# Hybrid encoder, two layers: the second half's leading products taken from unnormalised tiles

## The chip, the cores and the metric

The kernel runs on one core of one Trainium2 chip. The core has a matrix engine (TensorE, in profiles PE), three engines for elementwise work (VectorE or DVE, ScalarE or ACT, GpSimd or POOL) and a queue engine (SyncE or SP) that issues most transfers. The metric is the device time of one execution in microseconds (us). Results of TensorE land in PSUM, eight banks of 128 x 512 float32 values; everything else lies in SBUF.

## The reference

Two layers of an encoder over 512 tokens of width 1024. Each layer has a token-mixing part and a channel-mixing part, each behind an RMS norm and followed by one:

```python
mem_n = rms_norm(mem, mem_norm_g)
for l in range(DEPTH):
    h = rms_norm(x, g_pre_mix[l])
    proj = h @ w_in[l]
    q_a, k_a, v_a, q_b, k_b, v_b, q_m, gate_pre = jnp.split(proj, splits, axis=-1)
    # o_a: 2-D neighbourhood attention, 6 heads; o_b: dilated attention, 6 heads;
    # o_m: attention of q_m into (mem_n @ w_mem_kv[l])
    gates = jax.nn.sigmoid(gate_pre.reshape(B, S, N_BRANCH, D) + b_gate[l])
    merged = (gates[:, :, 0] * (o_a @ w_br_a[l]) + gates[:, :, 1] * (o_b @ w_br_b[l])
              + gates[:, :, 2] * (o_m @ w_br_m[l]))
    x = x + rms_norm(merged @ w_out[l], g_post_mix[l])
    h = rms_norm(x, g_pre_ffn[l])
    u = depthwise_conv_centred(h @ w_up[l], conv_w[l], conv_b[l])
    a, b = jnp.split(u, 2, axis=-1)
    f = jax.nn.gelu(a) * b
    x = x + rms_norm(f @ w_down[l], g_post_ffn[l])
```

RMS norm divides a token's 1024 values by the root of their mean square and multiplies by a gain per channel. The factor of the division is one number per token (the token factor); since it is constant over the channels that a product sums over, `(x * gain * factor) @ w` equals `((x * gain) @ w) * factor`.

## The kernel before

**Layout.** Activations are held transposed: channels on the 128 partitions, tokens along the free dimension. The residual `x` is eight k tiles of 128 x 512 in two constant tensors. Many steps work on one half of the tokens (256, `HALVES`) at a time.

**Products.** Every float32 operand is split into a rounded part (`hi`, made by ScalarE) and its remainder (`lo`, made by VectorE or POOL), and `mm3` (line 244) replaces one product by three matmuls: hi x hi, hi x lo, lo x hi. Weights arrive by SP as 512 KB pieces into `wraw` (three buffers) and are split by `weights` (line 222) into `whi` and `wlo` (two buffers each), or into smaller `m`, `h` or `ka` tiles where they have to lie ready earlier. All matmuls are recorded at line 242, all transposes at line 253, and all ScalarE and VectorE instructions at line 114, so the profile's groups are told apart by tile names.

**Order of the work.** TensorE's order is fixed by the program: each of its instructions is chained behind the one before (`Woven.pe`, line 56). A clock `wv.clk` adds an estimated cost to each; jobs are generators that wait until a due time on this clock or until a flag is given. `wv.tick` (line 83), called after each k tile of a product, runs the jobs that are due. So the places of a job's matmuls between those of the projections come from the planner's estimates; when the engines come later than these, TensorE waits in order. `ready` (line 183) is a delay taken from estimated end times of ScalarE and VectorE. The order of the other engines' instructions within their queues is set when the program is built, and can differ from the order in the code.

**Token factors.** `rstd_job` (line 321) multiplies the sums of squares by a column of 1/1024 (`pt<-mean,...`), takes root and reciprocal (`st`), and spreads the factors over all partitions by two float32 matmuls per half: a column of `st`, read 128 times over, against the identity (`pt<-ident,st`). It runs 18 times in the program.

**The end of layer 0 and the start of layer 1.** `sublayer_end` (line 779) does w_down; its last m tile is done half by half. After each half an `end_job` (line 373) normalises the result (`og`, multiplied by the factors), adds it to `x`, and sums the squares of the new `x`; then `pre_norm_job` (line 359) computes the token factors for layer 1, multiplies `x` by gain and factor, and splits the result into `h` tiles (`normed`, line 340). Beside these stand the memory's keys and values (`mem_kv`, line 444; the value job `mem_v_job` transposes into score banks `s`). The memory's own norm is `mem_norm_job` (line 416): four loads on ScalarE's queue, eight squares on ScalarE, seven adds on POOL in layer 1, one `rstd_job`, and eight `normed`. It is started at the end of layer 0's up-projection.

**The leading products.** Layer 1 begins with six projections of neighbourhood attention whose weights are prepared ahead (`FIRST`, line 28; q, k and v of the first two head pairs). `run_group` (line 466) takes them two banks at a time: `mm, mm`, then `s, s`, then `o, pt`, 48 matmuls of 128 x 256 a pair; first for half 0, as soon as its `h` tiles are there, then for half 1. After that the six banks are read out (`a_q`, `a_k`, `a_v`, lines 528 to 550) and the other projections follow with both halves at once (`proj`, line 480). `a_v` copies values into one buffer `sq`, one part by ScalarE, two narrow parts by VectorE; `v_job` transposes it.

**A second form of norm, in the channel mixing.** `factor_end_job` (line 388) already gives out tiles with the gain but without token factors (`raw_split`, line 345); the up-projection takes them, and the factors, kept in a tile `R`, are multiplied to the results when these leave PSUM (`scaled`, line 354).

Of the kernel before, what the change touches and what calls it, by code (L numbers as in the profile page):

```python
# [14 lines left out]
SEQ = 512  # L15
# [12 lines left out]
FIRST = (0, 3, 6, 1, 4, 7)  # L28
# [91 lines left out]
def tile_hybrid_encoder(ctx, tc, xT, memT, memg, vecs, rpb, w_in, w_kv, w_bra, w_brb, w_brm,  # L120
# [238 lines left out]
    def pre_norm_job(l, goff, acc, hs, i):  # L359
        half, box = HALVES[i], []  # L360
        yield from rstd_job(acc if isinstance(acc, list) else [acc[:, half]], 256, box)
        for k in range(KD):
            normed(x[k][:, half], vec[:, l, goff + k:goff + k + 1], box[0], hs[k][0][:, half], hs[k][1][:, half],
                   G if k in LOG[l > 0 and goff == V_PRE] else V)
        crit[0] = last_copy[0]
        yield 1.2
        wv.give(f"h{l}.{goff}.{i}")
# [5 lines left out]
    def end_job(l, goff, og, acc, acc2, i, then, lat, more=()):  # L373
        half, box = HALVES[i], []
        yield lat
        yield from rstd_job([acc[:, half]] + list(more), 256, box)
        for k in range(KD):
            V.tensor_mul(og[k][:, half], og[k][:, half], box[0])
            (G if then is None and i and k in TAILG else V).tensor_add(x[k][:, half], x[k][:, half], og[k][:, half])
            if acc2 is not None:  # L380
                sumsq_add(acc2[:, half], x[k][:, half], k == 0, None, G if k in SQG[goff == V_POSTF] else V)
            else:
                nc.sync.dma_start(out=out[:, k, half], in_=x[k][:, half])
        if then is not None:
            yield 9.0
            yield from then(i)

    def factor_end_job(l, goff, og, acc, acc2, i, nxt):
# [5 lines left out]
        for k in range(KD):  # L394
            V.tensor_mul(og[k][:, half], og[k][:, half], box[0])
            V.tensor_add(x[k][:, half], x[k][:, half], og[k][:, half])
            raw_split(l, gnext, k, x[k][:, half], h[k][0][:, half], h[k][1][:, half])
            if k == 0:
                yield 0.6
            wv.give(f"h{l}.{gnext}.{i}.{k}")  # L400
            yield 1.05
        for k in range(KD):
            sumsq_add(acc2[:, half], x[k][:, half], k == 0)
# [4 lines left out]
        if i == 1:  # L408
            yield 0.6
            wv.give(f"R{l}.{gnext}")  # L410

# [51 lines left out]
    def group_banks():  # L463
        return [mmbank(), mmbank(), sbank(), sbank(), obank(128), tbank()]

    def run_group(grp, hs, half, flag, cols=None, side=2):
        if flag and side == 2:
            wv.need(flag)
        n = len(hs)
        ws, pss = grp  # L470
        for i in range(0, len(ws), side):
            for k in range(n):
                if flag and side > 2:
                    wv.need(f"{flag}.{k}")
                rhs = [t[:, half] for t in hs[k]]
# [66 lines left out]
    def a_v(ps, qkv, flag):  # L542
# [5 lines left out]
        V.tensor_copy(vv[:, 0, :, 8:16], ps3[:, :, 0:8])  # L548
        V.tensor_copy(vv[:, 0, :, 0:8], ps3[:, :, 56:64])
# [229 lines left out]
    def sublayer_end(l, goff, w_of, rhs, n_half, then, lat=(1.4, 1.8), mid=None, fill=()):  # L779
# [26 lines left out]
        for i, half in enumerate(HALVES):  # L806
# [12 lines left out]
            if isinstance(then, tuple):  # L819
# [5 lines left out]
    def first_squares(half):  # L825
        sqs = [ytile((128, 256)) for _ in range(KD)]
        for k in range(KD):
            ACT.activation(sqs[k], x[k][:, half], AF.Square)
# [17 lines left out]
    hm = []  # L846
# [3 lines left out]
    for l in range(depth):  # L850
        pss = group_banks()
        for i in range(2):
            run_group((gw, pss), hs, HALVES[i], f"h{l}.{V_PRE}.{i}")
# [5 lines left out]
        for pr in range(3):  # L859
            for i, evac in enumerate((a_q, a_k, a_v)):  # L860
                ps = pss[3 * pr + i] if pr < 2 else proj(l, 3 * i + pr, hs, fence if i < 2 else None)
# [38 lines left out]
        for i in range(2):  # L900
            run_group((gw, list(pss.values())), hs, HALVES[i], f"h{l}.{V_PREF}.{i}", None, 4)
# [41 lines left out]
        else:  # L943
            hm, km, vm = [], [], []
            wv.spawn(mem_norm_job(l + 1, hm, htile))
            box, pre = [], []

            def then(a, i, l=l, box=box):
                if i == 0:
                    box.extend(h_tiles())  # L950
# [16 lines left out]
            sublayer_end(l, V_POSTF, w_of, fs, 1, then, (1.4, LAT1), lambda: wv.spawn(kv_ahead()))  # L967
# [38 lines left out]
def _layout(inputs):  # L1006
# [13 lines left out]
    a["xT"] = np.ascontiguousarray(g["x"][0].T.reshape(KD, 128, SEQ).transpose(1, 0, 2))  # L1020
# [46 lines left out]
```

## Time and profile before

| | |
|---|---|
| median of three runs | 1564.54 us (1564.0 to 1566.41) |
| profiled execution | 1565.1 us, its span 1563.3 us |
| TensorE busy, matmuls | 1524.4 us, 7994 |
| VectorE, ScalarE, POOL busy | 945.2, 735.1, 155.2 us |
| mean granted TensorE clock | 0.994 of full speed |
| read from memory | 141.47 MB, 92 GB/s over the span |

A profile row gives the start and the length in us, the engine, the line, the operation, the tile written and those read (buffer numbers left out), the shapes and how many instructions of this kind are merged; in square brackets stands the idle time just before, and what ended it. Matmuls are pipelined, so two rows can overlap: the distance from start to start is what one costs in a stream. A float32 matmul appears as two records. A group's row ends in "busy, mean ns of one | idle before".

### The profile page before, as it was taken

To read this page: it belongs to the slowest core of one execution; us is meant where nothing else is said; L and a number is where in the kernel's file an instruction comes from. 1 tells how busy PE (TensorE), PEld (TensorE's weight loads), DVE (VectorE), ACT (ScalarE), POOL (GpSimd) and SP (SyncE) were. 2 spreads that over 40 slices of the span, in tenths; PEclk is the share of its full clock that TensorE was granted. 3 is DMA by queue.
4 is the path that set the end of the run, shared out by engine and by line. 5 is a ranking of instruction groups with operands and counts; after the bars stand their busy time and mean duration, and the time that the engine had idled before them with its cause. 6 is when DMAs were issued, how large, how long until landed. Compare 5 with 4: busy or idle time off the path is not lost.

```text
span 1563.3 us, 20698 instructions
## 1 busy us (share of the span) xinstructions
PE 1524.4 (98%) x7994; PEld 1303.7 (83%) x7994; DVE 945.2 (60%) x1682; ACT 735.1 (47%) x1267; POOL 155.2 (10%) x219
## 2 busy tenths in 40 slices
PE   6999999999999999999989999999999999999997
PEld 6888888888988888788889888888889888888887
DVE  6685566235777777742385856753456877775233
ACT  5564575236544444522344645743364544444231
POOL 4340000210000000100061400001100000000000
PEclk9999999999999999999989999999999999999999
DMA  7222113325113322333331221132250222333331
GB/s 244 88 79 72 61 57 96 93 95 163 54 56 101 100 94 95 104 98 101 115 115 44 80 69 63 56 108 81 95 189 15 81 95 95 94 100 96 98 103 63
DMA packets 46610, 144.90 MB, mean 93 GB/s; under 512 B 5232, under 2 KB 11376, under 8 KB 46512
## 3 DMA queue, kind: packets, MB, share of 16 engines
q1 hardware_dynamic: 44656, 139.61, 28.2%
q10 hardware_dynamic: 1152, 2.10, 0.5%
q0 software_dynamic: 704, 1.88, 0.4%
q8 instruction: 62, 1.02, 0.3%
q14 instruction: 36, 0.29, 0.1%
HBM read 141.47 MB, written 2.10 MB: 92 GB/s over the span
## 4 chain that ended last, share of the span: by engine, by line
PE 54%; DVE 3%; issue 0%; ACT 0%; ACTq 0%; DVEq 0%
PE mm L242 48%; PE s L242 3%; PE o L242 2%; PE pt L242 1%; PE pt L253 1%; DVE y L114 1%; DVE x L114 1%; DVE m L114 0%; DVE acc L114 0%; DVE wlo L114 0%; DVE ka L114 0%; DVE st L114 0%; ACT sq L114 0%; ACT y L114 0%; ACT m L114 0%
## 5 line engine op out<-in xcount | busy, mean ns | idle before, releaser
L242 PE MATMUL mm<-h,whi 128*128 128x512 f32 x2496 | 775.7, 392 | 0.0
L242 PEld LDWEIGHTS mm<-h,whi 128*128 128x128 f32 x2496 | 461.5, 188 | 90.9
L242 PE MATMUL mm<-h,wlo 128*128 128x512 f32 x1248 | 486.4, 390 | 0.0
L114 DVE TENSOR_TENSOR wlo<-wraw,whi 128x1024 fp32r<-128x1024 f32 (+1 forms) x213 | 259.8, 1221 | 293.9 <-ACT whi L114 291.5
L114 ACT CAST whi<-wraw 128x1024 fp32r<-128x1024 f32 (+1 forms) x213 | 221.0, 1039 | 318.5 <-PE mm L242 310.4
L242 PEld LDWEIGHTS mm<-h,wlo 128*128 128x128 f32 x1248 | 234.3, 188 | 49.9
L242 PE MATMUL mm<-m,whi 128*128 128x512 f32 (+1 forms) x800 | 216.3, 358 | 2.7 <-ACT whi L114 1.8
L242 PEld LDWEIGHTS mm<-m,whi 128*128 128x128 f32 x800 | 142.5, 190 | 25.1 <-ACT whi L114 2.2
L242 PE MATMUL mm<-m,wlo 128*128 128x512 f32 (+1 forms) x400 | 142.8, 357 | 1.2 <-DVE wlo L114 1.2
L114 DVE SCALAR_TENSOR_TENSOR y<-y,vec,y 128x511 f32<-128x511 f32 x176 | 130.9, 750 | 3.5 <-ACT y L114 0.9
L114 DVE TENSOR_TENSOR y<-mm,R 128x512 f32<-128x512 f32 x82 | 56.4, 688 | 68.5 <-PE mm L242 68.5
L242 PEld LDWEIGHTS mm<-m,wlo 128*128 128x128 f32 x400 | 75.9, 190 | 12.5 <-DVE wlo L114 1.6
L766 POOL TENSOR_TENSOR m<-m,y 128x512 f32<-128x512 f32 x28 | 36.1, 1288 | 405.7 <-DVE y L114 405.7
L114 ACT ACTIVATE y<-y,vec 128x512 f32<-128x512 f32 x88 | 71.0, 813 | 2.2 <-DVE y L114 1.9
L242 PE MATMUL mm<-m,m 128*128 128x512 f32 x240 | 63.6, 395 | 0.0
L114 ACT ACTIVATE y<-y 128x512 f32<-128x512 f32 x44 | 27.8, 632 | 72.0 <-DVE y L114 71.5
L242 PE MATMUL s<-h,m 128*128 128x256 f32 x384 | 54.7, 290 | 5.4 <-DVE m L114 5.4
L114 ACT ACTIVATE y<-mm,vec 128x512 f32<-128x512 f32 (+1 forms) x91 | 57.4, 631 | 0.1
L242 PE MATMUL mm<-h,m 128*128 128x256 f32 x360 | 54.6, 298 | 2.8 <-DVE h L114 1.8
L114 ACT CAST m<-pt 128x512 fp32r<-128x512 f32 (+1 forms) x72 | 38.2, 539 | 40.4 <-PE pt L253 32.0
L114 DVE TENSOR_TENSOR acc<-acc,sq 128x256 f32<-128x256 f32 (+1 forms) x80 | 40.5, 507 | 26.2 <-ACT sq L114 24.6
L114 DVE TENSOR_TENSOR m<-pt,m 128x512 fp32r<-128x512 f32 (+1 forms) x72 | 45.0, 629 | 18.3 <-ACT m L114 17.4
(143 smaller groups left out, 1762.5 us busy)
## 6 DMA issues: line engine op xcount, KB each, us to landing
wraw<-in_w_in_dram SPq DMA_DIRECT2D x88, 512.0 KB, 3.4
wraw<-in_w_up_dram SPq DMA_DIRECT2D x88, 512.0 KB, 3.3
wraw<-in_w_down_dram SPq DMA_DIRECT2D x32, 512.0 KB, 3.5
wraw<-in_w_out_dram SPq DMA_DIRECT2D x16, 512.0 KB, 4.2
wraw<-in_w_down_dram SPq DMA_DIRECT2D x16, 384.0 KB, 3.1
wraw<-in_w_kv_dram SPq DMA_DIRECT2D x8, 512.0 KB, 4.4
wraw<-in_w_bra_dram SPq DMA_DIRECT2D x16, 192.0 KB, 2.3
x<-in_xT_dram SPq DMA_DIRECT2D x8, 256.0 KB, 6.9
```

The source lines that it names most:

```text
L114: return op(*args, **kw)
L242: wv.pe(nc.tensor.matmul(ps, a, b, start=first, stop=last), cost)
L253: wv.pe(nc.tensor.transpose(ps[:, 128 * i:128 * i + 128], s, ident), 0.11)
L766: (V if br == 2 and m >= 6 else G).tensor_add(acc[m], acc[m], gs)
```

## The change

1. `rstd_job` spreads the factors with TensorE's transposes of the same 128-fold read column, at a planned cost of 0.11 instead of 0.22.
2. In layer 1 the second half's leading products read raw tiles. A new `raw_end_job` replaces `end_job` and `pre_norm_job` for half 1 at the end of layer 0: it updates `x`, splits `x` times gain into eight raw tiles of the `ka` kind (of which there are 12 buffers), gives a flag for each, sums the squares afterwards, copies the spread factors to `R`, and then makes the normalised `h` tiles as before, since all further projections need them. After the group, six VectorE instructions multiply the second half of the six banks by `R` in PSUM.
3. The six leading projections come in another order, so that the pairs are `mm, mm`, then `o, pt`, then `s, s`. Each projection keeps its kind of bank.
4. `mem_norm_job` for layer 1 starts 20 us of the planner's clock later.
5. `a_v`'s two narrow copies move from VectorE to ScalarE.
6. `x` is one tensor, half by half; the input is laid out to match, so that a load reads 2 KB in a row from each partition instead of twice 1 KB.

```diff
-FIRST = (0, 3, 6, 1, 4, 7)
+FIRST = (0, 3, 4, 7, 6, 1)
...
-    xs = [const.tile([128, 4, 512], F32, name=f"x{i}") for i in range(2)]
-    x = [xs[k // 4][:, k % 4, :] for k in range(KD)]
+    xs = const.tile([128, 2, KD, 256], F32, name="x")
+
+    def xh(k, half):
+        return xs[:, half.start // 256, k, :]
...
-            nc.sync.dma_start(out=xs[k // 4][:, k % 4:k % 4 + 2, half], in_=xT[:, k:k + 2, half])
+            i = half.start // 256
+            nc.sync.dma_start(out=xs[:, i, k:k + 2, :], in_=xT[:, i, k:k + 2, :])
...
-            mm(pr[:, 128 * b:128 * b + 128], spread, ident, True, True, 0.22)
+            wv.pe(nc.tensor.transpose(pr[:, 128 * b:128 * b + 128], spread, ident), 0.11)
...
+    def raw_end_job(l, goff, og, acc, acc2, nxt, lat):
+        half, box = HALVES[1], []
+        hs, raw, R = nxt
+        yield lat
+        raw.extend((t[:, 0, :], t[:, 1, :]) for t in [ktile(F32R, (128, 2, 256)) for _ in range(KD)])
+        yield from rstd_job([acc[:, half]], 256, box)
+        for k in range(KD):
+            V.tensor_mul(og[k][:, half], og[k][:, half], box[0])
+            V.tensor_add(xh(k, half), xh(k, half), og[k][:, half])
+            raw_split(l + 1, V_PRE, k, xh(k, half), *raw[k])
+            if k == 0:
+                yield 0.6
+            wv.give(f"raw{k}")
+            yield 1.05
+        for k in range(KD):
+            sumsq_add(acc2[:, half], xh(k, half), k == 0)
+        yield 3.5
+        box = []
+        yield from rstd_job([acc2[:, half]], 256, box)
+        ACT.copy(R[:, half], box[0])
+        wv.give("R")
+        for k in range(KD):
+            normed(xh(k, half), vec[:, l + 1, V_PRE + k:V_PRE + k + 1], box[0], hs[k][0][:, half], hs[k][1][:, half])
+        crit[0] = last_copy[0]
+        yield 1.2
+        wv.give(f"h{l + 1}.{V_PRE}.1")
...
-        return [mmbank(), mmbank(), sbank(), sbank(), obank(128), tbank()]
+        return [mmbank(), mmbank(), obank(128), tbank(), sbank(), sbank()]
...
-        V.tensor_copy(vv[:, 0, :, 8:16], ps3[:, :, 0:8])
-        V.tensor_copy(vv[:, 0, :, 0:8], ps3[:, :, 56:64])
+        ACT.copy(vv[:, 0, :, 8:16], ps3[:, :, 0:8])
+        ACT.copy(vv[:, 0, :, 0:8], ps3[:, :, 56:64])
...
-        for i in range(2):
-            run_group((gw, pss), hs, HALVES[i], f"h{l}.{V_PRE}.{i}")
+        run_group((gw, pss), hs, HALVES[0], f"h{l}.{V_PRE}.0")
+        if l == 0:
+            run_group((gw, pss), hs, HALVES[1], f"h{l}.{V_PRE}.1")
+        else:
+            run_group((gw, pss), raw, FULL, "raw", HALVES[1], 2, True)
+            wv.need("R")
+            for ps in pss:
+                V.tensor_mul(ps[:, HALVES[1]], ps[:, HALVES[1]], R[:, HALVES[1]])
+            wv.need(f"h{l}.{V_PRE}.1")
...
-            wv.spawn(mem_norm_job(l + 1, hm, htile))
+            wv.spawn(mem_norm_job(l + 1, hm, htile), 20.0)
...
-            sublayer_end(l, V_POSTF, w_of, fs, 1, then, (1.4, LAT1), lambda: wv.spawn(kv_ahead()))
+            sublayer_end(l, V_POSTF, w_of, fs, 1, [then, (box, raw, R)], (1.4, LAT1), lambda: wv.spawn(kv_ahead()))
```

What is left out carries the new forms of `x` and of the flags through the other functions.

More of the change, by code (lines that the diff above doesn't have):

```diff
@@ L362, in pre_norm_job @@
         for k in range(KD):
-            normed(x[k][:, half], vec[:, l, goff + k:goff + k + 1], box[0], hs[k][0][:, half], hs[k][1][:, half],
+            normed(xh(k, half), vec[:, l, goff + k:goff + k + 1], box[0], hs[k][0][:, half], hs[k][1][:, half],
                    G if k in LOG[l > 0 and goff == V_PRE] else V)
@@ L378, in end_job @@
             V.tensor_mul(og[k][:, half], og[k][:, half], box[0])
-            (G if then is None and i and k in TAILG else V).tensor_add(x[k][:, half], x[k][:, half], og[k][:, half])
+            (G if then is None and i and k in TAILG else V).tensor_add(xh(k, half), xh(k, half), og[k][:, half])
             if acc2 is not None:
-                sumsq_add(acc2[:, half], x[k][:, half], k == 0, None, G if k in SQG[goff == V_POSTF] else V)
+                sumsq_add(acc2[:, half], xh(k, half), k == 0, None, G if k in SQG[goff == V_POSTF] else V)
             else:
-                nc.sync.dma_start(out=out[:, k, half], in_=x[k][:, half])
+                nc.sync.dma_start(out=out[:, k, half], in_=xh(k, half))
         if then is not None:
@@ L402, in factor_end_job @@
         for k in range(KD):
-            sumsq_add(acc2[:, half], x[k][:, half], k == 0)
+            sumsq_add(acc2[:, half], xh(k, half), k == 0)
         yield 3.5
@@ L463, in group_banks, with run_group @@
     def group_banks():
-        return [mmbank(), mmbank(), sbank(), sbank(), obank(128), tbank()]
-    def run_group(grp, hs, half, flag, cols=None, side=2):
-        if flag and side == 2:
+        return [mmbank(), mmbank(), obank(128), tbank(), sbank(), sbank()]
+    def run_group(grp, hs, half, flag, cols=None, side=2, each=False):
+        each = each or side > 2
+        if flag and not each:
             wv.need(flag)
@@ L472, in run_group @@
             for k in range(n):
-                if flag and side > 2:
-                    wv.need(f"{flag}.{k}")
-                rhs = [t[:, half] for t in hs[k]]
+                if flag and each:
+                    wv.need(f"{flag}{k}")
+                rhs = [t[:, half] if half != FULL else t for t in hs[k]]
                 for w, ps in zip(ws[i:i + side], pss[i:i + side]):
@@ L818, in sublayer_end @@
                         post_norm_tile(l, goff, m, ps, og, acc, half, n0 == 0 and len(order) + len(pair) == KD and m == pair[0])
-            if isinstance(then, tuple):
+            if isinstance(then, list) and i:
+                wv.spawn(raw_end_job(l, goff, og, acc, acc2, then[1], lat[1]))
+            elif isinstance(then, list):
+                wv.spawn(end_job(l, goff, og, acc, acc2, 0, lambda i: then[0](acc2, i), lat[0]))
+            elif isinstance(then, tuple):
                 wv.spawn(factor_end_job(l, goff, og, acc, acc2, i, then))
@@ L827, in first_squares @@
         for k in range(KD):
-            ACT.activation(sqs[k], x[k][:, half], AF.Square)
+            ACT.activation(sqs[k], xh(k, half), AF.Square)
             if k % 2:
@@ L900, in tile_hybrid_encoder @@
         for i in range(2):
-            run_group((gw, list(pss.values())), hs, HALVES[i], f"h{l}.{V_PREF}.{i}", None, 4)
+            run_group((gw, list(pss.values())), hs, HALVES[i], f"h{l}.{V_PREF}.{i}.", None, 4)
         fs, held, flag = [], [], f"R{l}.{V_PREF}"
@@ L1019, in _layout @@
     a = {}
-    a["xT"] = np.ascontiguousarray(g["x"][0].T.reshape(KD, 128, SEQ).transpose(1, 0, 2))
+    a["xT"] = np.ascontiguousarray(g["x"][0].T.reshape(KD, 128, 2, 256).transpose(1, 2, 0, 3))
     a["memT"] = np.ascontiguousarray(g["mem"][0].T.reshape(KD, 128, N_MEM).transpose(1, 0, 2))
```

12 lines of the change are left out of this document (6 added, 6 removed).

## The prediction

> **What bounds the kernel now.** I read the busy shares first, then what TensorE waits for, then the time line at each of those waits.
>
> ```profile
> span 1563.3 us, 20698 instructions
> ...
> PE 1524.4 (98%) x7994; PEld 1303.7 (83%) x7994; DVE 945.2 (60%) x1682; ACT 735.1 (47%) x1267; POOL 155.2 (10%) x219
> ```
>
> TensorE is idle for 1563.3 - 1524.4 = 38.9 us. A gain is either a removed wait of TensorE or less work on it; time on the other engines counts only where TensorE waits for it.
>
> ```profile
> PE pt L242 <- DVE y L114: 9.0, 1, 9.0
> PE s L242 <- DVE m L114: 5.4, 1, 5.4
> PE pt L253 <- DVE sq L114: 2.4, 2, 1.3
> PE mm L242 <- ACT whi L114: 1.8, 1, 1.8
> PE pt L242 <- DVE acc L114: 1.4, 1, 1.4
> ...
> PE mm L242 <- DVE wlo L114: 1.2, 1, 1.2
> ```
>
> The 9.0 is the start of the kernel. The 5.4 and the 1.4 lie between the layers; the 1.8 and the 1.2 lie together at the end of layer 0's up-projection; the two waits at `sq` are the value transposes.
>
> **The wait at 661 us.** Time line of TensorE, then of POOL, ScalarE and VectorE, and the chain of waits in layer 1's channel mixing:
>
> ```profile
> 661.06 0.39 PE L242 MATMUL mm<-m,wlo 128*128 128x512 f32 x1
> 663.26 0.74 PE L242 MATMUL mm<-m,whi 128*128 128x512 f32 x2 [1.81 <-ACT whi L114]
> 665.20 0.50 PE L242 MATMUL mm<-m,wlo 128*128 128x512 f32 x1 [1.20 <-DVE wlo L114]
> ...
> 671.24 0.62 PE L242 MATMUL mm<-m,whi 128*128 128x512 f32 x2
> ...
> 671.92 0.62 PE L242 MATMUL mm<-ka,whi 128*128 128x512 f32 x2
> ```
> ```profile
> 658.28 7.45 POOL L316 TENSOR_TENSOR h<-h,sq 128x256 f32<-128x256 f32 x7 [301.60 <-ACT sq L114]
> ```
> ```profile
> 662.17 1.77 ACT L114 CAST whi<-wraw 128x1024 fp32r<-128x1024 f32 x2
> ```
> ```profile
> 663.38 3.17 DVE L114 TENSOR_TENSOR wlo<-wraw,whi 128x1024 fp32r<-128x1024 f32 x2
> ```
> ```profile
> 1213.91 324.66 PE mm L242 x1500
> ```
>
> One k tile takes 671.92 - 671.24 = 0.68 us. From 661.29 (661.06 + a third of 0.68) to 671.92 eight k tiles ran, worth 5.44 us, in 10.63: the place costs 5.2 us, 3.0 of waiting and 2.2 of slower matmuls. ScalarE is late with `whi` while POOL adds the memory squares. Layer 1 has the same code without memory squares, and its chain runs through this place as 1500 matmuls without a break. So the memory squares make the wait.
>
> **The wait at 807 us, between the layers.** Time lines of TensorE and VectorE, and four-microsecond windows (PEclk is the third column from the end):
>
> ```profile
> 791.52 0.58 PE L242 MATMUL pt<-mean,acc 128*128 128x1 f32 x4 [1.43 <-DVE acc L114]
> ...
> 802.88 0.71 PE L242 MATMUL pt<-ident,st 128*128 128x128 f32 x4
> ...
> 807.01 0.52 PE L242 MATMUL s<-h,m 128*128 128x256 f32 x3
> 812.91 7.13 PE L242 MATMUL s<-h,m 128*128 128x256 f32 x45 [5.37 <-DVE m L114]
> ...
> 832.27 5.92 PE L242 MATMUL s<-h,m 128*128 128x256 f32 x48
> 838.03 0.52 PE L242 MATMUL o<-h,m 128*128 128x256 f32 x3
> ...
> 843.79 0.63 PE L242 MATMUL mm<-h,whi 128*128 128x512 f32 x2
> ...
> 851.31 0.60 PE L253 MATMUL pt<-ident,sq 128*128 128x128 f32 x4
> ```
> ```profile
> 803.63 0.75 DVE L114 TENSOR_TENSOR y<-y,pt 128x256 f32<-128x256 f32 x2 [0.16 <-PE pt L242]
> ...
> 812.35 0.41 DVE L114 TENSOR_TENSOR m<-s,m 128x256 fp32r<-128x256 f32 x1
> ...
> 815.97 1.30 DVE L114 TENSOR_TENSOR acc<-acc,sq 128x256 f32<-128x256 f32 x2 [0.20 <-ACT sq L114]
> ```
> ```profile
> 792.00:796.00 4.00, 4.00 (x22) 4.00 (x23) 2.56 (x8) 1.60 (x5) 3.88 (x8) 0.57 0.15 24
> ...
> 812.00:816.00 4.00, 3.09 (x14) 3.12 (x15) 3.79 (x12) 1.31 (x4) 0.65 (x2) 0.50 0.51 164
> ```
>
> The leading products are pairs of banks; 48 matmuls take 838.03 - 832.27 = 5.76 us, 0.12 each. At 807.01 the first score bank is written; the second is still being read by the memory values' split, which VectorE ends at 812.35 + 0.41 = 812.76, and TensorE goes on at 812.91. After this wait and after the one of 1.43 us the granted clock is 0.50 and 0.57; the 45 matmuls behind the first took 7.13 where 45 x 0.12 and a tail of 0.16 (5.92 - 5.76) make 5.56, so the slow clock costs 1.6. From the spread at 802.88 to the end of the group at 843.79 lie 126 + 144 = 270 matmuls (18 of the first half's 144 come ahead of it), 32.4 us, and three small groups of 0.36; the measured 40.9 us hold 7.4 too many.
>
> **The change, part by part.**
>
> (a) The memory job starts 20 us later. Its eight squares, seven POOL adds and four loads on ScalarE's queue move among the w_down tiles; its mean and spread stay ahead of their use, which comes behind the last w_down tile. Gain at most 5.2. At the new place a set of eight k tiles lasts 5.44 us, and its cast and subtraction 0.9 + 1.6 (half of 1.77 and of 3.17), so 2.9 us are to spare, while POOL's adds last 7.45 and ScalarE's last squares wait for them. Least gain 1.0 if a wait of that size appears with the slower matmuls behind it; I take 4.0, near the upper end, because the ScalarE queue there no longer has the GELU work.
>
> The row of 3.17 us for two subtractions has POOL's adds beside it. The Trainium skill (SBUF — State Buffer, "SBUF: two separate sides") calls the port pair that VectorE and GpSimd share an exclusive lock that one holds for its whole instruction. It speaks against the move: the lock travels with the adds. By the rule alone up to 7.45 - 2.9 = 4.5 us of the lock surface and (a) is under 1 (rival B); by layer 1's rows, which have no adds, it is near 5.
>
> (b) Second-half products from the raw tiles, and the pair on the `o` and `pt` banks ahead of the score banks. The pair order takes the wait away: TensorE reaches the score banks at 802.88 + 0.36 + 78 x 0.12 = 812.6, against 812.76 for the split. The planner puts the second mean 0.6 + 8 x 1.05 + 3.5 us after the spread; it steps once in six matmuls, so this becomes 138 matmuls, and TensorE is there at 802.88 + 0.2 + 16.6 = 819.7. VectorE's last sum of squares ended at 817.27; the eight new `lo` instructions stand before it:
>
> ```profile
> L114 DVE SCALAR_TENSOR_TENSOR h<-x,vec,h 128x256 fp32r<-128x256 f32 x32 | 15.1, 483 | 0.0
> ```
>
> 8 x 0.483 = 3.9, less if they overlap as pairs do, so 820.4 to 821.2: a wait of about 0.9. The normalised tiles are still needed for the other projections: eight steps of a multiplication (0.48 at most, as `lo`) and a subtraction (0.41, as at 812.35), 7.1 us, behind root and spread, some 2. Before, TensorE took the first of them up at once; now it has 132 matmuls, 15.8 us, behind that mean, so 9.1 us of chain are hidden. Without that cover the 9.1 would be a wait. The six bank multiplications cost 0.38 each (803.63: two in 0.75), 2.3 in all on VectorE; four are hidden by the last pairs, two end 0.8 after the group, under the next projection, whose third `mm` bank is free. If that cover went, 0.8 us. Eight of twelve `ka` buffers are held by the raw tiles until the last pair; the second key's zero borders on POOL wait for them, two heads ahead of their use; behind these in POOL's queue stand the first key's copies for head 0. Of 7.4 I subtract 0.9 for the mean and 1.0 for the split, which stands in the VectorE queue that has grown: 5.5. Ends: 7.4, and -0.3 (rival A).
>
> The 1.43 us wait was followed by a clock of 0.57. The Trainium skill (TensorE: Matmul & The Clock Gate, "The HAM clock gate") has half rate only after an idle window of about 3.4 us; the trace does not agree. By the rule a wait of 0.9 costs just that; by the row 1.6 more is possible.
>
> (c) Spreads by transposes. Groups of instructions and the time line:
>
> ```profile
> L242 PE MATMUL pt<-ident,st 128*128 128x128 f32 x72 | 12.4, 298 | 1.8 <-DVE st L114 1.8
> ```
> ```profile
> 779.08 0.60 PE L242 MATMUL pt<-ident,st 128*128 128x128 f32 x4
> 779.44 0.48 PE L242 MATMUL mm<-m,whi 128*128 128x256 f32 x2
> ...
> 862.65 0.60 PE L253 MATMUL pt<-ident,y 128*128 128x128 f32 x4
> 863.00 0.71 PE L242 MATMUL mm<-h,whi 128*128 128x512 f32 x2
> ```
>
> A float32 spread is two records, a transpose one. Two spreads hold TensorE for 0.36, four transposes for 0.35: 0.18 saved per job, 72/4 = 18 jobs, 3.2 us. Ends: 1.6 if half lies in waits, 3.3.
>
> (d) Loading x. Waits of the first 60 us, and one-microsecond windows (GB/s last):
>
> ```profile
> ACT y L114 <- DMA x<-in_xT_dram: 3.9, 3, 2.3
> ```
> ```profile
> 2.00:3.00 1.00, 0.00 (x0) 0.00 (x0) 0.00 (x0) 0.23 (x2) 1.00 (x3) 1.00 0.94 301
> ...
> 8.00:9.00 1.00, 0.00 (x0) 0.00 (x0) 0.85 (x2) 0.69 (x2) 0.00 (x0) 1.00 1.01 401
> ```
>
> Rows of 1 KB become 2 KB. 1.05 MB take 3.5 us at 301 (x) and 2.6 at 401 (weights, 4 KB rows): at most 0.9, least -0.2; I take 0.4.
>
> (e) The value job's two narrow copies go to ScalarE, and the planner's estimate of VectorE grows by six multiplications, so it places the transposes (now 851.31 - 843.79 = 7.5 us behind the group) some 1.5 us later, and with them each attention head. Hidden by the projections unless these run out (then 1.5, and 0.7 if ScalarE is late as well, which makes the lower end -2.2; the upper one, +0.4, is a shorter wait at `sq`, now 2.4 in two); I take -0.6.
>
> Sum: 4.0 + 5.5 + 3.2 + 0.4 - 0.6 = 12.5. The profiled execution took 1565.1 and the median is 1564.54, 0.6 less: 1565.1 - 12.5 - 0.6 = 1552.0.
>
> **The rivals.**
>
> A. *The longer VectorE queue takes the wait's place.* The split slips by some 2.4 us (five or six `lo` ahead of it) and the last sum by 2.1 past TensorE, each with 1.6 of slow matmuls: 7.4 - 4.0 - 3.7 = -0.3, total 6.7, 1557.8. For it: VectorE is busy for 3.79 of the 4 us from 812, and both margins are under 1 us. Against it: `lo` instructions can fill gaps in which VectorE waited for POOL.
>
> B. *The memory sums bring their wait along.* POOL's adds stretch the subtractions of weights and hold ScalarE's last squares at the new place as at the old one: (a) is 0, the sum 8.5, 1556.0. For it: 7.45 us of adds against 2.9 to spare. Against it: at 661 the GELU's products and the split of its result stood in the same queues, and among the w_down tiles little else does. The lock of the Trainium skill named under (a) is this rival's rule.
>
> C. *Slower: the value copies on ScalarE.* Three copies in a row behind casts of weights. Each of six value jobs has transposes in TensorE's fixed order; the two waits there now sum to 2.4. It decides from some 2.1 us of new loss at each of the six (12.5 / 6); at 3.2 (1.6 wait, 1.6 slow clock) it takes 19.2: 1571.2. Against it: only two of six waited at all.
>
> D. *The change doesn't do what it says:* A and B together, only the spreads and little else remain: 1565.1 - 2.7 - 0.6 = 1561.8.
>
> **How the numbers follow.** Forecast 0.55, A 0.17, B 0.12, D 0.09, C 0.07. The forecast's own range is 1548.9 to 1556.5 (a between 2 and 5.2, b between 3 and 7.4). All upper ends together give 1547.3, all lower ends 1564.6; 1547 to 1559.5 takes in A and B. 0.2% is 3.1 us, about what a measurement here can tell from no change. Faster by more: forecast, A, B and 0.03 of D, 0.87; within: 0.06 of D; slower: C, 0.07.
>
> **What would show it.** (a): no wait for `whi` at 661, none new among the w_down tiles. (b): `o` and `pt` products ahead of `s`, no wait for the split, second mean near 820 less what (a) saves, group end some 5 to 7 us nearer to its spread. (c): 36 spread records fewer. (e): waits at `sq` still under 1.5. The forecast is wrong if TensorE's waits between the layers still sum to over 4 us, if a wait over 2 us stands among the w_down tiles, or if the attention stage of layer 1 is longer by over 2 us.

## The result and the profile after

The changed kernel takes 1556.34 us (median of four runs, 1555.38 to 1556.76) where the kernel before takes 1564.89 in the same comparison: the ratio is 0.9944 with a 95% interval of 0.9926 to 0.9961. That is 8.5 us faster; 12.5 were forecast (1552.0, range 1547 to 1559.5).

The head of the profile's page and TensorE's waits after (us in total, times, longest):

```profile
span 1554.7 us, 20656 instructions
...
PE 1519.6 (98%) x7958; PEld 1299.5 (84%) x7958; DVE 951.5 (61%) x1684; ACT 739.8 (48%) x1288; POOL 152.9 (10%) x219
```
```profile
PE pt L245 <- DVE y L114: 10.3, 3, 8.1
...
PE pt L245 <- DVE acc L114: 4.6, 2, 3.4
PE pt L256 <- DVE y L114: 3.1, 3, 2.1
PE pt L256 <- ACT sq L114: 1.7, 2, 0.9
```

The waits for the bank `s` (5.4), for `whi` (1.8) and for `wlo` (1.2) are gone. In their place stand a longer wait for `acc` (4.6 in two; 1.4 before) and one of 2.1 for `y`, which the kernel before did not have. At the start of the kernel the first wait is shorter (8.1, 9.0 before), but two more follow it (10.3 in three). Busy time alone fell by only 4.8 us.

To see where the time went, I laid the same places of the two time lines of TensorE beside each other. Before, beyond the rows shown above:

```profile
655.84 0.61 PE L242 MATMUL mm<-m,whi 128*128 128x512 f32 x2
...
777.56 0.50 PE L242 MATMUL pt<-mean,acc 128*128 128x1 f32 x4
...
1023.77 0.59 PE L253 MATMUL pt<-ident,y 128*128 128x128 f32 x2 [0.47 <-DVE y L114]
```

After:

```profile
654.03 0.62 PE L245 MATMUL mm<-m,whi 128*128 128x512 f32 x2
...
770.32 0.50 PE L245 MATMUL pt<-mean,acc 128*128 128x1 f32 x4
...
771.83 0.38 PE L340 MATMUL pt<-ident,st 128*128 128x128 f32 x2
...
786.08 0.99 PE L245 MATMUL pt<-mean,acc 128*128 128x1 f32 x4 [3.44 <-DVE acc L114]
...
799.24 0.43 PE L340 MATMUL pt<-ident,st 128*128 128x128 f32 x2
...
817.37 0.58 PE L245 MATMUL pt<-mean,acc 128*128 128x1 f32 x4 [1.19 <-DVE acc L114]
...
832.97 0.63 PE L245 MATMUL mm<-h,whi 128*128 128x512 f32 x2
...
841.84 0.60 PE L256 MATMUL pt<-ident,sq 128*128 128x128 f32 x4
...
876.91 0.55 PE L256 MATMUL pt<-ident,y 128*128 128x128 f32 x3 [2.13 <-DVE y L114]
...
1016.58 0.59 PE L256 MATMUL pt<-ident,y 128*128 128x128 f32 x2 [0.48 <-DVE y L114]
```

| place | before | after | ahead by | since the last place |
|---|---|---|---|---|
| first w_down row | 655.84 | 654.03 | 1.8 | +1.8 |
| half 0, first mean behind w_down | 777.56 | 770.32 | 7.2 | +5.4 |
| half 0, second mean | 791.52 | 786.08 | 5.4 | -1.8 |
| half 1, spread | 802.88 | 799.24 | 3.6 | -1.8 |
| end of the leading group | 843.79 | 832.97 | 10.8 | +7.2 |
| late in layer 1's attention | 1023.77 | 1016.58 | 7.2 | -3.6 |
| end of the span | 1563.3 | 1554.7 | 8.6 | +1.4 |

So the two large gains came, 5.4 us where (a) acts (4.0 forecast) and 7.2 in the leading group (5.5 forecast for (b)), but two stretches give back 3.6 us each: half 0's second mean with the slow matmuls behind it, and the third head of layer 1. Four-microsecond windows of the first (PEclk third from the end):

```profile
784.00:788.00 4.00, 1.92 (x9) 1.95 (x10) 3.21 (x9) 2.66 (x9) 1.45 (x4) 0.72 0.36 131
788.00:792.00 4.00, 4.00 (x21) 4.00 (x21) 2.94 (x9) 1.16 (x3) 1.61 (x5) 0.50 0.00 0
```

What makes that mean late stands in the time lines of POOL and VectorE from 770 us on, after:

```profile
770.80 6.91 POOL L223 TENSOR_TENSOR m<-wraw,m 128x512 fp32r<-128x512 f32 x5 [105.58 <-ACT m L114]
779.10 4.25 POOL L223 TENSOR_TENSOR m<-wraw,m 128x512 fp32r<-128x512 f32 x3 [1.38 <-ACT m L114]
```
```profile
775.05 0.74 DVE L114 TENSOR_TENSOR y<-y,pt 128x256 f32<-128x256 f32 x2
...
779.36 1.41 DVE L114 TENSOR_TENSOR acc<-acc,sq 128x256 f32<-128x256 f32 x1
...
784.22 0.41 DVE L114 TENSOR_TENSOR acc<-acc,sq 128x256 f32<-128x256 f32 x1
```

and in POOL's before:

```profile
778.05 5.48 POOL L220 TENSOR_TENSOR m<-wraw,m 128x512 fp32r<-128x512 f32 x4 [112.32 <-ACT m L114]
783.48 0.38 POOL L536 CAST ka<-zero 128x8 fp32r<-128x8 f32 x1
```

Before, POOL's eight weight subtractions ran four together and four with the zero borders of the next keys (`ka<-zero`) between them, and the last two (from 791.72) began behind the second mean. After, the borders wait for the raw tiles to leave the `ka` buffers, and all eight subtractions lie ahead of the second mean, which comes 14.25 us after the spread (771.83 to 786.08; 12.44 before). An addition of VectorE takes 0.41 us at 784.22, when POOL is done, and 1.41 at 779.36, when it meets one of them. Products with a PSUM operand (`y<-y,pt`, 0.74 for two) are not stretched. The Trainium skill (SBUF — State Buffer, "SBUF: two separate sides") states just this: a VectorE instruction with two SBUF inputs and a POOL instruction that reads SBUF exclude each other. The trace agrees, 0.41 against 1.41 us.

My theory at this point: (a), (b) and (c) are worth what was forecast, and what is missing is the 1.8 us of chain (14.25 - 12.44) with the slow clock behind it, which comes from the borders (H1), and the third head's wait, an accident of the plan (H2). The rivals: the order of pairs alone earns (b); the raw tiles cost by their own work; the single terms are mis-sized.

### The profile page after: what moved, and what is told of

It reads as the page before. It is cut to its first block, busy times and chain, and to the rows that moved or that the text cites. A ratio compares the mean times of both kernels' runs of the same rounds, so it can differ in the third digit from the quotient of the medians.

```text
span 1554.7 us, 20656 instructions
## 1 busy us (share of the span) xinstructions
PE 1519.6 (98%) x7958; PEld 1299.5 (84%) x7958; DVE 951.5 (61%) x1684; ACT 739.8 (48%) x1288; POOL 152.9 (10%) x219
## 4 chain that ended last, share of the span: by engine, by line
PE 91%; DVE 6%; ACT 2%; issue 1%; DMA 0%; SPq 0%; ACTq 0%; DVEq 0%
PE mm L245 80%; PE s L245 4%; PE o L245 3%; PE pt L256 2%; DVE y L114 1%; DVE m L114 1%; PE pt L245 1%; DVE x L114 1%; DVE ka L114 1%; ACT y L114 1%; DVE acc L114 1%; DVE wlo L114 0%; ACT m L114 0%; DMA x<-in_xT_dram 0%; DVE h L114 0%
## 5 line engine op out<-in xcount | busy, mean ns | idle before, releaser
L245 PEld LDWEIGHTS mm<-m,wlo 128*128 128x128 f32 x400 | 75.5, 189 | 10.8
L114 ACT ACTIVATE y<-y,st 128x256 f32<-128x256 f32 (+1 forms) x80 | 43.6, 547 | 27.0 <-DVE st L114 26.8
L114 ACT CAST m<-y 128x512 fp32r<-128x512 f32 x32 | 19.8, 620 | 72.5 <-DVE y L114 72.5
```

What stands on the lines that cost most here:

```text
L114: return op(*args, **kw)
L245: wv.pe(nc.tensor.matmul(ps, a, b, start=first, stop=last), cost)
```

## The experiments

Each run is compared with the kernel before on the same chip, five rounds; medians, ratio and 95% interval are of those. An interval is about 2 us to either side (0.0012 x 1565), and 2.7 for the changed kernel, so a difference between two kernels is told from zero from some 3 us on. The runs were made on several chips, so where median and ratio differ, the ratio is the fairer figure. One thing lies across all comparisons with the changed kernel: at the first w_down row its profiled execution (654.03) is 1.2 to 1.4 us behind those of most runs below (652.6 and 652.8 in the first two), in code that is the same. This is its clock, which was granted in full at the same place in all the others:

```profile
24.62:28.03 3.41, 3.41 (x19) 3.41 (x18) 1.52 (x4) 1.57 (x5) 1.53 (x2) 0.50 0.74 222
```

Where I compare time lines I therefore count from a place behind that row.

**The memory norm job at once.**

```diff
-            wv.spawn(mem_norm_job(l + 1, hm, htile), 20.0)
+            wv.spawn(mem_norm_job(l + 1, hm, htile))
```

> The changed kernel, but the memory norm job is put into the plan at once again and not 20 us later; all else stays. Theory (the landmarks of the two traces): the wait of TensorE at the end of the feed-forward part, gone in the changed kernel, comes back, since ScalarE again takes the memory squares ahead of the copies that w_down waits for: 5.2 us slower than the changed kernel, near 1561.5 us, and a wait for ka in front of the w_down rows between 650 and 675. Rival (the wait went because the other buffers and pairs moved the plan, not because of the 20 us): within 1 us of the changed kernel, near 1556.

Measured: 1559.25 us, ratio 0.9971 (0.9959 to 0.9983): 2.9 us slower than the changed kernel (4.2 by the ratios). TensorE's time line:

```profile
652.61 0.61 PE L245 MATMUL mm<-m,whi 128*128 128x512 f32 x2
...
660.03 0.73 PE L245 MATMUL mm<-m,whi 128*128 128x512 f32 x2 [1.82 <-ACT whi L114]
...
773.98 0.50 PE L245 MATMUL pt<-mean,acc 128*128 128x1 f32 x4
```

The wait for `whi` is back, and from the first w_down row to the first mean lie 121.4 us where the changed kernel has 116.3 (770.32 - 654.03): 5.1 us, the whole place. The theory holds. How it works differs from what I had thought. The memory additions have not moved; ScalarE's queue of the changed kernel:

```profile
655.68 1.03 ACT L114 CAST whi<-wraw 128x1024 fp32r<-128x1024 f32 x1
...
656.93 1.32 ACT L114 ACTIVATE sq<-h 128x256 f32<-128x256 f32 x4
```
```profile
657.41 7.81 POOL L319 TENSOR_TENSOR h<-h,sq 128x256 f32<-128x256 f32 x7 [301.79 <-ACT sq L114]
```

One cast of weights now stands ahead of the squares; before, both casts stood behind them (1.77 at 662.17), and in this run they do again (1.78 at 658.94). That is the difference at this place.

**Normalised tiles with the new order of pairs.** The second half's leading products take `h` tiles as in the kernel before; raw tiles and bank products are left out.

```diff
-        if l == 0:
+        if True:
             run_group((gw, pss), hs, HALVES[1], f"h{l}.{V_PRE}.1")
...
-            sublayer_end(l, V_POSTF, w_of, fs, 1, [then, (box, raw, R)], ...)
+            sublayer_end(l, V_POSTF, w_of, fs, 1, then, ...)
```

> The changed kernel with its new order of pairs, but the leading products of the second half between the layers take normalised tiles as before, so the raw tiles and the factors multiplied to the banks are left out of it. Theory one (the raw tiles earn the 7.2 us at the second half, and cost 1.8 us of VectorE time in the first half by holding the buffers whose zero borders spaced out GpSimd's subtractions): the second half loses some 4 to 6 us, the first half's wait of 3.44 us falls back to about 1.4 us, 1558 to 1560 us. Rival (the new order of pairs alone does it, since the wait for an s bank is what went): 1553 to 1556 us. Second rival (raw tiles earn it all and cost nothing): 1562 to 1563 us, and the wait of 3.44 us stays.

Measured: 1550.20 us, ratio 0.9914 (0.9900 to 0.9928): 6.1 us faster than the changed kernel, faster than any of the three theories had it (some 1.2 of it may be the start's). TensorE:

```profile
769.12 0.50 PE L245 MATMUL pt<-mean,acc 128*128 128x1 f32 x4
...
782.99 0.58 PE L245 MATMUL pt<-mean,acc 128*128 128x1 f32 x4 [1.55 <-DVE acc L114]
...
807.50 0.58 PE L245 MATMUL pt<-mean,acc 128*128 128x1 f32 x4 [2.18 <-DVE acc L114]
...
1009.65 0.59 PE L256 MATMUL pt<-ident,y 128*128 128x128 f32 x2 [0.47 <-DVE y L114]
```

There is no wait at a score bank, and none at the third head. All that the raw tiles save is 2.18 - 1.19 = 1.0 us at half 1's mean and a wait of 0.3 at an `h` tile behind it. Counted from the first mean, the second comes 1.9 us earlier (13.87 against 15.76), and the late row in the attention 5.7 us earlier (240.53 against 246.26).

**The old order of pairs, with either kind of tile.**

```diff
-FIRST = (0, 3, 4, 7, 6, 1)
+FIRST = (0, 3, 6, 1, 4, 7)
...
-        return [mmbank(), mmbank(), obank(128), tbank(), sbank(), sbank()]
+        return [mmbank(), mmbank(), sbank(), sbank(), obank(128), tbank()]
```

> The changed kernel without both halves of part (b): the second half's leading products take normalised tiles, and the pairs stand in the old order mm, mm / s, s / o, pt. Only one thing sets it apart from the run with normalised tiles and the new order (1550.2 us). Theory (the order of the pairs alone took away the 5.37 us in which TensorE waited for an s bank): that wait comes back at the first s product of the first half, and the time is 1555 to 1556.5 us; if the third head's transposes fall behind VectorE as well, some 4 us more. Rival (the gain of that run came from the zero borders and the memory norm job, not from the order): within 1.5 us of 1550.2.

> The changed kernel with raw tiles as they are, but the pairs in the old order mm, mm / s, s / o, pt. Theory (the raw tiles do nothing for the first half, where the s bank is late): the wait for an s bank comes back with 4 to 5.5 us, 1560 to 1562 us. Rival (the raw tiles alone give the gain of part (b)): 1556 us or less, with no wait at an s bank over 1 us.

Measured: normalised 1555.49, ratio 0.9942 (0.9930 to 0.9954); raw 1559.73, ratio 0.9973 (0.9963 to 0.9984). The two in turn:

```profile
803.60 7.74 PE L245 MATMUL s<-h,m 128*128 128x256 f32 x45 [5.27 <-DVE m L114]
```
```profile
805.83 7.65 PE L245 MATMUL s<-h,m 128*128 128x256 f32 x45 [5.40 <-DVE m L114]
```

| us | old order | new order |
|---|---|---|
| normalised tiles | 1555.5 | 1550.2 |
| raw tiles | 1559.7 | 1556.3 |

The order earns 3.4 to 5.3 us and removes the wait for the bank with either kind of tile. The raw tiles cost 4.2 to 6.1 us, of which some 1.2 may be the start's. By the ratios the order earns 4.4 and 4.5 us and the raw tiles cost 4.7 and 4.9, so the two hardly act on each other. The change without (b) (1555.5) is as fast as the change (1556.3).

**POOL's subtractions apart.** Raw tiles stay; six tiny copies stand behind each subtraction of the first two leading weights.

```diff
+        if spaced and eng is G:
+            behind(last_lo[G], spaced[0])
+            for _ in range(6):
+                spaced[0] = nc.gpsimd.tensor_copy(scratch, lo[:, 0, 0:8]).ins
```

> The changed kernel with six tiny copies on GpSimd behind each of the four subtractions for the leading groups' first two weights, so that these stand apart as the zero borders had them stand apart in the kernel before. Theory one (VectorE's additions take 1.4 to 1.8 us in place of 0.41 us because GpSimd's subtractions run beside them back to back): the chain from spread to mean falls from 14.25 us to 12.0 to 12.8 us, the wait of 3.44 us to 1.0 to 2.0 us, 2 to 4 us faster, 1552.5 to 1554.5 us. Rival (the chain is longer for the order of VectorE's own queue, and GpSimd has no part in it): within 0.5 us of 1556.3 us.

Measured: 1551.15 us, ratio 0.9916 (0.9902 to 0.9929): 5.2 us faster than the changed kernel by doing more work. POOL, then TensorE:

```profile
769.37 6.91 POOL L224 TENSOR_TENSOR m<-wraw,m 128x512 fp32r<-128x512 f32 x5 [105.58 <-ACT m L114]
776.34 2.07 POOL L228 CAST scratch<-m 128x8 fp32r<-128x8 f32 x6
```
```profile
783.50 0.58 PE L250 MATMUL pt<-mean,acc 128*128 128x1 f32 x4 [2.32 <-DVE acc L114]
```

The wait fell from 3.44 to 2.32 and the chain from 14.25 to 13.1 us: the direction of H1, though less than I had expected. From the first mean (768.88) to the value transposes (837.81) lie 68.9 us where the changed kernel has 71.5 (841.84 - 770.32): 2.6 of the 5.2 are shown at this place, 1.1 as waiting and the rest as a faster clock behind it; 1.4 are ahead of w_down.

**The borders late, with normalised tiles.** The reverse: the best kernel so far, with only POOL's border casts put behind its last subtractions, as the raw tiles force them to be.

```diff
-            nc.gpsimd.tensor_copy(t[:, 0:8], zero)
-            nc.gpsimd.tensor_copy(t[:, 520:528], zero)
+            behind(nc.gpsimd.tensor_copy(t[:, 0:8], zero).ins, last_lo.get(G) if wv.clk > 400 else None)
+            behind(nc.gpsimd.tensor_copy(t[:, 520:528], zero).ins, last_lo.get(G) if wv.clk > 400 else None)
```

> The kernel with the new order of pairs and normalised tiles (1550.2 us; it leaves the raw tiles out), with GpSimd's zero borders of the second layer's keys put behind its last subtractions, where the raw tiles push them in the changed kernel. TensorE's, VectorE's and ScalarE's orders are untouched. Theory (the raw tiles cost the first half its time through these borders): the chain from spread to second mean grows from 12.35 us to 13.3 to 14.3 us, the wait there from 1.55 us to 2.5 to 3.5 us, 1.5 to 4 us slower, 1551.7 to 1554 us. Rival (the raw tiles' own splits and bank products cost it): the wait stays at 1.55 us, within 0.5 us of 1550.2.

Measured: 1554.74 us, ratio 0.9927 (0.9914 to 0.9940): 4.5 us slower than its partner by the medians, 2.0 by the ratios, whose intervals overlap: the total is not told from zero, but the rows of POOL and TensorE are clear.

```profile
769.27 6.92 POOL L223 TENSOR_TENSOR m<-wraw,m 128x512 fp32r<-128x512 f32 x5 [105.58 <-ACT m L114]
777.56 4.25 POOL L223 TENSOR_TENSOR m<-wraw,m 128x512 fp32r<-128x512 f32 x3 [1.38 <-ACT m L114]
```
```profile
784.54 0.99 PE L245 MATMUL pt<-mean,acc 128*128 128x1 f32 x4 [3.44 <-DVE acc L114]
```

These are the rows of the changed kernel to a hundredth: 6.92 and 4.25 us of subtractions, a wait of 3.44, and 15.76 us from the first mean to the second. The order of the instructions is its partner's on TensorE, VectorE and ScalarE. Without a raw tile in the kernel, the moved borders alone make the loss at half 0's second mean. H1 is shown from both sides. (That raw tiles cost nothing more by holding these buffers was not measured apart: a kernel with the raw tiles in the `m` buffers gave no time, since it deadlocks.)

**The second mean later.** `yield 9.0` in `end_job` becomes `yield 12.0`.

> The changed kernel, but the second sum of squares of the first half between the layers is put 3 us later in TensorE's order (12 in place of 9). Theory one (VectorE's chain sets the start of the leading products whatever TensorE does meanwhile): the 3.44 us wait at the mean becomes under 0.6 us, but the memory products then end early, and 2 us or so of waiting stand at the first leading products for the tiles of the first half: 1 to 2 us faster, near 1555 us. Rival (the misplaced mean alone costs it: its wait and the slow clock behind it): both go, and 4 to 6 us with them, 1550.5 to 1552.5 us.

Measured: 1558.14 us, ratio 0.9953 (0.9940 to 0.9966): no gain; both theories missed. TensorE:

```profile
785.18 6.07 PE L245 MATMUL mm<-h,m 128*128 128x256 f32 x27 [3.53 <-ACT y L114]
```

The same 3.5 us are spent ahead of the memory products that now stand in front of the mean. What those products wait for the profile names ScalarE's `y`. That row (`y<-mm,vec`) reads an `mm` bank from 784.66 to 785.13, just ahead of the products; ScalarE reaches it only behind squares that waited 3.04 and 0.59 us for VectorE's `x`. So the wait is still that for VectorE's queue, at another place, and another of 2.05 us follows at the next spread. Moving the mean alone doesn't remove it.

**The third head.** With the spaced subtractions, the first transposes of layer 1's third head are planned 2 us later.

```diff
-            yield LAT_QK if bp == 0 else ready(LAT_SM)
+            yield LAT_QK if bp == 0 else ready(LAT_SM) + (2.0 if (l, h) == (1, 2) else 0.0)
```

> The changed kernel with the spaced subtractions (1551.2 us by themselves) and the third head's first transposes of the second layer put 2 us later in TensorE's order. Theory (the 2.13 us wait there and the slow clock behind it, 3.6 us together, come from a plan that places these transposes ahead of VectorE's queue): both go, 3 to 4 us off, 1547 to 1548.5 us, below the kernel with normalised tiles. Rival (VectorE is the bound in that stretch and the wait moves to the next products): 1550 to 1551.5 us.

Measured: 1550.09 us, ratio 0.9909 (0.9895 to 0.9924), against 0.9916 without. No row of TensorE waits at the third head's transposes; a new one follows close by:

```profile
876.13 0.63 PE L261 MATMUL pt<-ident,sq 128*128 128x128 f32 x4 [0.67 <-DVE m L114]
```

By the time lines 2.8 us are gained between the value transposes and the late row in the attention; by the medians 1.1, which the intervals do not separate. The wait goes as the theory had it, but the time is the rival's. The wait itself goes with the plan; every profile with raw tiles and the old plan has it (1.43 to 2.29 us), none with normalised tiles has. Why the raw tiles bring it is open. With them the orders of TensorE and of VectorE differ from those with normalised tiles in this stretch; that the six bank products do it, by lengthening the planner's estimate for VectorE, is my guess.

**The value copies back on VectorE,** once in the changed kernel, once with normalised tiles, where TensorE's order stays the same:

```diff
-        ACT.copy(vv[:, 0, :, 8:16], ps3[:, :, 0:8])
-        ACT.copy(vv[:, 0, :, 0:8], ps3[:, :, 56:64])
+        V.tensor_copy(vv[:, 0, :, 8:16], ps3[:, :, 0:8])
+        V.tensor_copy(vv[:, 0, :, 0:8], ps3[:, :, 56:64])
```

> The changed kernel with the two narrow copies of the first group's values back on VectorE. Theory one (the third head's transposes wait 2.13 us because the later value products shifted the plan against VectorE's queue): the 2.13 us wait and the slow clock behind it go, 3 to 4 us faster than the changed kernel, 1552.5 to 1553.5 us. Theory two (the wait there hangs on the raw tiles, since it was absent with normalised tiles): 1556.5 to 1558.5 us, the copies' own 0.6 to 2.2 us coming back.

> The kernel with the new order of pairs and normalised tiles (1550.2 us; it leaves the raw tiles out), with the narrow value copies back on VectorE; here TensorE's order stays what it is, so that the copies alone are measured. Theory (on ScalarE they save what the rows showed, a wait of 0.85 in place of 1.10 us and of 0.80 in place of 1.29 us): 0.5 to 1.0 us slower, 1550.7 to 1551.2 us. Rival (the 2.6 us that the same edit gained on the changed kernel are the copies' own): 1547.5 to 1548.5 us.

Measured: 1553.73, ratio 0.9932 (0.9918 to 0.9945), 2.6 us faster than the changed kernel; 1552.55, ratio 0.9919 (0.9908 to 0.9931), 2.4 us slower than its own partner by the medians and 0.8 by the ratios. With opposite signs and overlapping intervals (e) is not told from zero. In the first run the third head's wait is 1.43 and not 2.13, and no slow clock follows it: the time is near theory one's, but the wait has not gone as that theory had it. In the second, TensorE's waits are its partner's but for the value transposes (1.29 and 1.11 us for 0.80 and 0.85); the rest of the difference is in the clock, as the last section shows.

**Spreads as float32 products.**

```diff
-            wv.pe(nc.tensor.transpose(pr[:, 128 * b:128 * b + 128], spread, ident), 0.11)
+            mm(pr[:, 128 * b:128 * b + 128], spread, ident, True, True, 0.22)
```

> The changed kernel with the factors spread by float32 matrix products against the identity again, in place of transposes. Theory (each of 18 spreads is 0.18 us longer on TensorE, and none is hidden): 3.2 us slower, 1559.5 us. Rival (half of them stand ahead of waits for VectorE that begin no later): 1.6 us slower or less, 1556.5 to 1558 us.

Measured: 1563.16 us, ratio 0.9992 (0.9983 to 1.0001): 6.8 us slower, twice the theory. By the ratios it is 7.5. The spreads of the changed kernel (there are 72 records of them here), and this kernel's means:

```profile
L340 PE MATMUL pt<-ident,st 128*128 128x128 f32 x36 | 7.8, 300 | 1.1 <-DVE st L114 1.1
```
```profile
771.96 0.50 PE L245 MATMUL pt<-mean,acc 128*128 128x1 f32 x4
...
788.82 0.98 PE L245 MATMUL pt<-mean,acc 128*128 128x1 f32 x4 [4.33 <-DVE acc L114]
...
821.16 0.58 PE L245 MATMUL pt<-mean,acc 128*128 128x1 f32 x4 [2.70 <-DVE acc L114]
...
848.13 0.60 PE L256 MATMUL pt<-ident,sq 128*128 128x128 f32 x4
```

From half 0's first mean to the value transposes lie 76.2 us where the changed kernel has 71.5 (841.84 - 770.32). Four of the 18 spreads stand there, worth 0.7; the waits at the two second means grew by 0.9 and 1.5, and a slower clock follows the second. A spread heads a chain of VectorE work, so its own 0.2 us can count again where the chain's end is waited for, but 0.9 and 1.5 are more than that. VectorE's queue also comes in another order here: at half 0's chain POOL's subtractions group six and two, not five and three, and two additions (`x<-x,y`, from 778.14) take 2.94 us where the changed kernel's (from 776.48) take 1.84. How much of the 6.8 is the spreads' length and how much the new order was not measured apart.

**Both repairs of the chain at once:** normalised tiles, and the spacing copies (the two diffs above together).

> The kernel with the new order of pairs and normalised tiles (1550.2 us) with the spacing copies on GpSimd added; it leaves the raw tiles out. Theory (each subtraction on GpSimd that runs within the chain costs VectorE 0.8 to 1.1 us, and two of them stand in the later half of the chain): one moves out behind it, the wait of 1.55 us falls to 0.5 to 1.0 us, 0.5 to 1.5 us faster, 1548.7 to 1549.7 us. Rival (what is left of that chain is VectorE's own work): within 0.4 us of 1550.2.

Measured: 1553.42 us, ratio 0.9933 (0.9920 to 0.9945): 3.2 us slower than the normalised kernel. TensorE:

```profile
781.80 0.58 PE L250 MATMUL pt<-mean,acc 128*128 128x1 f32 x4 [0.83 <-DVE acc L114]
...
809.65 0.58 PE L250 MATMUL pt<-mean,acc 128*128 128x1 f32 x4 [2.75 <-DVE acc L114]
```

The first wait fell to 0.83 as the theory had it. But the subtractions pushed out of that chain now lie later: TensorE waits 1.28 and 1.24 us for the factors (`st`) at the next two spreads (0.40 and none in its partner), and 2.75 for 2.18 at the next mean. From half 0's first mean to that row it takes 41.0 us, 2.6 more than its partner: the gain was more than given back. The order of TensorE, VectorE and ScalarE is its partner's.

The best kernels are the one with normalised tiles and the new order (1550.20) and the one with raw tiles, spaced subtractions and the moved head (1550.09): 14.8 and 14.5 us below the kernel before by their own comparisons, and some 6 below the changed kernel.

## Why the prediction was right, and where it was not

The time came within the range, on the slow side, but the sum is right in part by luck: (b) was worth nothing that can be told from zero where 5.5 were forecast, and (c) some 3.6 more than its 3.2 by the medians. The time itself doesn't tell the forecast from its rivals either: 1556.3 lies nearest to rival B's 1556.0, and B's mechanism was not seen. What was seen as forecast: no wait for `whi` and no wait at the score bank, a wait of 1.19 for 0.9 at the second mean, and 36 spread records fewer. Two of the three signs that it named for being wrong appeared: the waits between the layers still sum to over 4 us (3.44 + 1.19), and the attention stage is over 2 us longer. By its steps:

(a) *The memory job*: 4.0 forecast; 5.1 at the place, 2.9 in the medians. The size was right, the mechanism not: I had the squares and additions move among the w_down tiles and a new wait appear for want of 2.9 us of room. They stayed at the same time (657.41, 658.28 before); ScalarE's queue changed by one cast. So rival B, which let the additions bring their wait along, had nothing to act on.

(b) *Raw products and the order of pairs*: 5.5 forecast, and the leading group did get shorter by 7.2 us. "The pair order takes the wait away" is shown by the run with normalised tiles. The wait of about 0.9 at the second mean came as 1.19. The step that failed is the one on the `ka` buffers: "the second key's zero borders on POOL wait for them, two heads ahead of their use". I looked at who needs the borders and costed their delay at nothing; I didn't ask what would run on POOL in their place. Two more subtractions came into VectorE's chain, and three ran without borders between them (1.8 us of chain, and 6.8 us at half clock behind a wait of 3.44, for 3.4 us behind one of 1.43). With the third head's wait the raw tiles cost 4.2 to 6.1 us, and (b) as a whole is worth -0.8 us (1555.5 - 1556.3; -0.3 by the ratios), not told from zero. The gain of (b) is its order of pairs, 3.4 to 5.3 us.

Rival A, a longer VectorE queue in the wait's place, was right in kind and wrong in place and cause: not the `lo` instructions of half 1, but stretched additions of half 0.

(c) *The spreads*: 3.2 forecast with ends of 1.6 and 3.3; 6.8 measured. The term counted only TensorE's own time. It left out what the edit does to the waits behind the spreads, 2.4 us at the two second means alone; whether by the spreads' length or by VectorE's changed order stays open.

(d) *Loading x*: 0.4 forecast. It was not undone by itself; the kernel with float32 spreads shares the new load and the old spreads. The first `mm<-m,whi` row with a wait for `m` starts at 63.28 us there and at 63.25 in the kernel before, which would leave nothing for the load. But the kernels of this document that share load, spreads and value copies with the changed one reach that row anywhere from 60.35 to 61.70 us, and the changed one, behind its half clock, at 62.55, so one execution of each cannot settle 0.4 us. The term is neither shown nor refuted.

(e) *The value copies*: -0.6 forecast, not told from zero. The sign that would make the forecast wrong, "the attention stage of layer 1 is longer by over 2 us", did appear (3.6), but through the third head and not through the value jobs, whose waits are 0.9 each. Rival C did not happen.

The single effects do not add up to the total: each is measured behind others, and waits, chains and clock share the same few places.

## What to carry to other kernels

When an instruction is delayed at no cost to those who need it, ask what then runs in its slot: here 24 trivial casts kept GpSimd's subtractions off VectorE, and six tiny copies behind each of four of them, which do nothing, bought 2.6 us back at that place. Added to the kernel that already had the casts, the same copies made the next waits longer: what matters is what runs beside the chain that is waited for. Where a change bundles a reordering and a mechanism, take them apart first: the reordering of six products earned all that the raw tiles seemed to. For a shorter instruction at the head of a chain, look at the wait at the chain's end too: by its own length it was worth about half of what was measured here.

## What the runs showed of the hardware

A wait of the same length is followed by a slow TensorE in one execution and not in another. The kernel with normalised tiles and the same with the value copies on VectorE have the same order of TensorE's instructions and the same wait of 1.55 us at half 0's second mean, from 781.44 to 782.99 and from 780.99 to 782.54. The first two windows are of the former, the other two of the latter:

```profile
778.97:782.38 3.41, 2.47 (x21) 2.26 (x19) 3.24 (x8) 1.31 (x5) 3.41 (x10) 1.00 0.03 7
782.38:785.79 3.41, 2.40 (x19) 2.23 (x20) 2.42 (x7) 2.15 (x8) 3.41 (x9) 1.00 0.42 149
```
```profile
781.10:784.51 3.41, 1.76 (x13) 1.59 (x13) 2.62 (x8) 2.19 (x7) 3.41 (x12) 1.00 0.45 154
784.51:787.92 3.41, 3.22 (x15) 3.22 (x16) 3.02 (x9) 1.16 (x3) 3.23 (x7) 0.50 0.38 101
```

The edges of these windows are the places where the clock can change. In all 14 traces every change of the clock between the start and the end of the kernel lies on a grid of 3.41 us that keeps its phase through an execution and has a phase of its own in each, and a half clock lasts one or two stretches of it. In the first execution the wait is cut by a grid line at 782.38, and TensorE is busy for 2.47 and 2.40 us of the two stretches. In the second nearly all of it falls into one stretch, TensorE is busy for 1.76 us of it, and the next stretch runs at half clock. Counted over all stretches at full clock in the 14 traces: behind each of the 20 in which TensorE's rows fill less than 1.4 us the clock is half, behind none of those over 2.1 us, and behind 8 of the 11 in between. So the same wait can cost its length alone or, as an estimate, up to 1.7 us more for each stretch at half clock (half of 3.41), and which of them depends on where the grid lies in that execution. Single differences of that size between medians shouldn't be read as an edit's. The Trainium skill (TensorE: Matmul & The Clock Gate, "The HAM clock gate") has the activity watched in windows that run free of the kernel, and the grid agrees with that; that half rate needs a window of some 3.4 us of idleness the rows do not bear out.
